# Plain w2 products in the first half-step, and modulation tiles with fixed places

## The chip, the cores and the metric

The kernel runs on one core of a Trainium2 chip. The metric is the time of one execution on the device, in microseconds. The engines are TensorE (PE, with its weight loads as PEld), VectorE (DVE), ScalarE (ACT), GpSimd (POOL, hardly used here) and SyncE (SP), whose queue issues nearly all transfers (DMAs), one after the other.

## What is computed

One layer of a diffusion trunk on 640 tokens (512 latent, 128 prompt), width D = 1024, in fp32:

```python
def swiglu(h, w1, w3, w2):
    return (silu(h @ w1) * (h @ w3)) @ w2                # F = 2816

m = (silu(cvec) @ w_ada + b_ada).reshape(-1, 9, D)       # nine modulation vectors, for c and c_ctx
x = x + 0.5 * m[2] * swiglu(rmsnorm(x, g[0]) * (1 + m[1]) + m[0], w1a, w3a, w2a)
h = rmsnorm(x, g[1]) * (1 + m[4]) + m[3]
p = h @ w_in                                             # q, k, v of attention and mLSTM, gates gm, gd
y = sigmoid(gm) * (mlstm(p) @ w_br_m) + sigmoid(gd) * (diff_attention(p) @ w_br_d)
x = x + m[5] * (y @ w_out)
x = x + 0.5 * m[8] * swiglu(rmsnorm(x, g[2]) * (1 + m[7]) + m[6], w1b, w3b, w2b)
```

The new keys and values and the final mLSTM states of the prompt are outputs too.

## The kernel before

**Numbers.** Every fp32 operand of a product is split into a high part (ACT copies it to a shorter type, `wH`, `hH`) and the rest (DVE subtracts, `wL`, `hL`), and a product is three matmuls: H x H, H x L, L x H. Tokens come in two halves of 320 (`HALF`, index `hf`), D in 8 blocks of 128, F in 11 blocks of 256 (`FB`).

**Half-steps.** After a start (norm, modulation m0 and m1, block 0 in plain products), 20 granules take blocks 1 to 10 of w1 and w3 ("up"), then 12 granules take w2 in three groups of blocks (`GROUPS`), four parts j of 256 output channels each ("down"). Every granule is a 2 x 2 product of blocks, done with 7 products instead of 8 (`HalfStep.products`): `Granule.parts` and `sums` make sums of weights (`raw<-raw`) and their splits (`wB`, `wC`, `ww`), `operand_sums` made sums of tokens, and `store_g` makes four sums of the gated tokens (`SO<-SO`), splits seven operands in two pieces (`g`, 128x1280 and 128x960) and stores them to `g_dram`, from where the down stage fetches them (`S`, `hm`, `op`) into places that become free. PE takes the products in the order in which they are written. The order of DVE, ACT and SP is made by a scheduler from that of the program and its own estimate of times; each of these engines then works strictly in its order.

**Modulation.** A vector m of 1024 channels is 8 tiles: a transfer `raw_a` of 128 x 1024 columns of w_ada, two dot products on DVE with silu(c) and silu(c_ctx) (`csil`; "ISA" or CUSTOM_DVE with a READ_ACCUMULATOR behind it), and the addition of `b_ada`. 24 tiles (m2 to m4) belong in the first half-step: 14 whole ones in the up stage (`modulation`, i = 4 to 17), 10 as two halves of 512 columns (`HalfColumns`) in the down stage, one transfer at a time. Twelve are in the attention, 12 in the branch products (`d_evac` and `m_evac`, once for each evacuated unit with mt = 1 in the first, once for each granule in the second), 8 (m8) in the second half-step (`modulation2`). The mixing's norm scale (`scale`, from m4) waits for all of the first 24.

**Mixing.** After the sum of squares (`ps_ss`) the modulated tokens go to `hH`, `hL` by block k, and PE begins with `ps_t` and `ps_g`. In the mLSTM, cells alternate with units of other products (`fill`), whose weights come through a ring of two buffers (tag `raw`) and are split a granule ahead. `w_brd`, `w_brm` (branch products, `ps_p`) and `w_out` follow; weights and modulation tiles share the ring there.

Of the kernel before, what the change touches and what calls it, by code (L numbers as in the profile page):

```python
# [16 lines left out]
D = 1024  # L17
# [14 lines left out]
def tile_trunk(ctx: ExitStack, tc: tile.TileContext, a: dict):  # L32
# [5 lines left out]
    def tt(eng, out, in0, in1, op):  # L38
        eng.tensor_tensor(out=out, in0=in0, in1=in1, op=op)  # L39
# [183 lines left out]
    GROUPS = ((0, 3), (3, 7), (7, FB))  # L223

# [3 lines left out]
    class Granule:  # L228
# [12 lines left out]
        def parts(self, fp, b12=False):  # L241
# [4 lines left out]
            E = [(self.two(fp, "C", 512, 3), hi[:, :nk])] if b12 else []  # L246
            for (h, lw), v in [(B, lo), (C, hi[:, nk:]), *E]:
# [9 lines left out]
            for i, t, o in [(A11, B, 0), (A12, B, nk * 128), (S4, C, 0), *(("b12", t, 0) for t, _ in E)]:  # L257
                self.w[i] = [[w[:, o + 128 * k : o + 128 * k + 128] for k in range(nk)] for w in t]
# [9 lines left out]

    class HalfStep:
        def __init__(self, n, fp, tmp, psum, w1, w3, w2):  # L270
# [4 lines left out]
            self.g_dram = dp.tile([7, 128, 2, FB, HALF], F32, name=f"g_dram{n}")  # L275
# [14 lines left out]
        def begin_gated(self):  # L290
            self.SO = self.fp.tile([128, 8, HALF], F32, tag="SO", name="SO")
# [4 lines left out]
        def gate_plain(self, f, hf, p):  # L296
            s = self.silu_tile(f, hf)
            act(s, p[0], AF.Silu)
            tt(vec, self.SO[:, Q[f, hf]], p[1], s, ALU.mult)
# [27 lines left out]
        def store_g(self, SO, b):  # L327

            tt(vec, SO[:, S1], SO[:, A21], SO[:, A22], ALU.add)
# [3 lines left out]
            for tag, c0, c1 in (("gA", 0, 4), ("gB", 4, 7)):  # L333
                g = self.fp.tile([128, 2, c1 - c0, HALF], F32R, tag=tag, name="g")
                act(g[:, 0], SO[:, c0:c1], AF.Copy)
                tt(vec, g[:, 1], SO[:, c0:c1], g[:, 0].bitcast(F32), ALU.subtract)
                for i in range(2):
                    nc.sync.dma_start(out=self.g_dram[c0:c1, :, i, b, :].rearrange("s p n -> p s n"), in_=g[:, i].bitcast(F32))


        def into(self, p, A, gr, i, first, w=None):

            wH, wL = gr.w[i if w is None else w]
# [10 lines left out]
        def products(self, work, between, tokens_early):  # L354
# [9 lines left out]
            for i, (gr, A, done, used) in enumerate(work):  # L364
                last = i + 1 == n

                def into(p, op, first, w=None, gr=gr, A=A, used=used):
                    self.into(p, A, gr, op, first, w)
                    if w is None:
                        used(op)  # L370

                if i + 2 < n:
                    work[i + 2][0].load()
                if not last:
                    work[i + 1][0].parts(self.fp, tokens_early and i + 2 == n)
# [4 lines left out]
                if last and tokens_early:  # L380
                    into(Z, A11, True, "b12")
                    tail[0]()
                    into(X, A12, False)
                    done(0, 0, X, None)
                    into(Z, A12, False, S4)
                    done(1, 0, Z, None)
                    tail[1]()
                    into(Y, S2, False)
                    into(Y, S3, False)
                    u3 = copy_of(Y, "nry")  # L390
                    V = acc_tile(psum)
                    into(V, S1, True)
                    done(1, 1, V, u3)
                    into(Y, A22, False)
                    done(0, 1, Y, None)
                    break
                into(Z, S1, True)
                if last:
                    p5 = copy_of(Z, "nt", 2)
                if tail:  # L400
                    tail[0]()
                if not last:
                    work[i + 1][0].sums()
                into(Y, S2, False)
# [32 lines left out]
        def up_done(self, b):  # L437
# [3 lines left out]
            def of_w1(f, hf, p, u):  # L441
                box[f, hf] = s = self.silu_tile(f, hf)
                if u is not None:
                    tt(vec, s, p, u, ALU.add)
# [3 lines left out]
            def of_w3(f, hf, p, u):  # L448
# [5 lines left out]
                tt(vec, box["SO"][:, Q[f, hf]], p, box[f, hf], ALU.mult)  # L454
                if (f, hf) == (1, 0):
# [4 lines left out]
        def run(self, x, gate, final, between, emptied=lambda: None, tokens_early=False):  # L460


            work = []
            for b in range(1, FB):
                for gr, done in zip(self.up[2 * b - 2 : 2 * b], self.up_done(b)):
                    work.append([gr, lambda i: self.ops[i], done, lambda i: None])
# [45 lines left out]
            def fetch_w2(b0, b1, j):  # L512
                def f(raw):
                    n = b1 - b0
                    for h in range(2):
                        dma(raw[:, h * n : (h + 1) * n], self.w2[b0:b1, :, h, 256 * j : 256 * j + 256].rearrange("b p n -> p b n"))
                return f

            for q, (b0, b1) in enumerate(GROUPS):
                for j in range(4):  # L520
                    work.append([Granule(b1 - b0, fetch_w2(b0, b1, j)), lambda i, q=q: at[q, i], *down_done(q, j)])
            self.products(work, between, tokens_early)


    csil_dram = dp.tile([2, D], F32, name="csil_dram")

# [1389 lines left out]
```

## Time and profile before

| | us |
|---|---|
| median of 3 runs (lowest, highest) | 1951.49 (1950.27, 1955.31) |
| profiled execution | 1950.12 |
| its span, of which PE busy | 1948.3, 1811.4 |
| first half-step up, from block 1 | 77.44 to 340.69 |
| first half-step down | 340.69 to 503.33 |
| wait of PE at the passage to the mixing | 32.5 |
| branch products | 1325.5 to 1391.5 |

The profiled execution is one of the kind that the median is made of; 1.8 us of it lie around the span. Matmuls of PE are pipelined, so a busy PE need not be PE at its best; where it is, shows in the number of matmuls that fit into a stretch.

### The profile page before, as it was taken

The page shows a single profiled execution, that of the slowest core. Times are in us where ns is not written, and L with a number is a line of the kernel's source. Part 1 is how long each engine was busy: PE and PEld are TensorE (multiplying, and loading weights), DVE is VectorE, ACT ScalarE, POOL GpSimd, SP SyncE. Part 2 cuts the span into 40 slices and gives each one's busy share as a digit, 9 for nine tenths or more (in the row PEclk, how much of TensorE's full clock was granted, in tenths as well). Part 3 has the DMA queues.
Part 4 walks back from the last instruction along what each step waited for, and adds up shares of the span by engine and source line. Part 5 has one row for each costly group of instructions (what it writes and reads, how often), then busy time and mean ns, then how long its engine had stood idle before and what let it go on. Part 6 is the DMA issues. An engine that isn't in the chain of part 4 may idle for free.

```text
span 1948.3 us, 30989 instructions
## 1 busy us (share of the span) xinstructions
PE 1811.4 (93%) x12502; PEld 1768.4 (91%) x12502; DVE 1419.9 (73%) x2480; ACT 899.1 (46%) x1537; POOL 4.9 (0%) x6
## 2 busy tenths in 40 slices
PE   6988999899398999999999989999899999999989
PEld 4888999889398998999999988899899999999989
DVE  7999888877668675675664535676666999887875
ACT  5644555433254354454453436555234545554432
POOL 1000000000000000000000000000000000000000
PEclk9899999999799999999999999999999999999999
DMA  8357555966424232133121243446643356557962
GB/s 316 138 194 241 200 179 199 396 235 220 151 78 149 69 110 94 66 104 111 67 101 59 95 163 119 142 137 225 226 143 131 113 208 233 178 181 257 385 230 100
DMA packets 144289, 328.42 MB, mean 169 GB/s; under 512 B 10321, under 2 KB 102225, under 8 KB 131345
## 3 DMA queue, kind: packets, MB, share of 16 engines
q1 hardware_dynamic: 144146, 326.44, 48.0%
q8 instruction: 98, 1.61, 0.3%
q14 instruction: 45, 0.37, 0.1%
HBM read 249.01 MB, written 77.39 MB: 168 GB/s over the span
## 4 chain that ended last, share of the span: by engine, by line
PE 68%; DVE 14%; DMA 9%; ACT 3%; issue 3%; SPq 0%; DVEq 0%; ACTq 0%
PE ps_f L52 29%; PE ps_p L52 17%; PE ps_t L52 11%; DMA raw_a<-in_w_ada_c 5%; PE sc L52 2%; PE ps_o L52 2%; DVE raw_a L559 2%; PE ps_n L52 2%; DVE raw L39 1%; DVE ww L39 1%; DMA S<-g_dram 1%; PE ps_wT L55 1%; PE ps_u L52 1%; DVE wB L39 1%; DVE junk L559 1%
## 5 line engine op out<-in xcount | busy, mean ns | idle before, releaser
L52 PE MATMUL ps_f<-S,ww 128*128 128x320 f32 x1944 | 318.7, 312 | 28.3 <-DVE ww L39 18.8
L52 PEld LDWEIGHTS ps_f<-S,ww 128*128 128x128 f32 x1944 | 295.4, 190 | 31.7 <-DVE ww L39 20.8
L52 PE MATMUL ps_p<-hH,wH 128*128 128x320 f32 x864 | 276.0, 319 | 9.7 <-DVE y L39 7.2
L52 PE MATMUL ps_p<-hL,wH 128*128 128x320 f32 x864 | 269.0, 311 | 0.0
L52 PE MATMUL ps_p<-hH,wL 128*128 128x320 f32 x864 | 268.7, 311 | 0.0
L52 PE MATMUL ps_t<-wH,hH 128*128 128x256 f32 x640 | 186.0, 291 | 32.5 <-ACT hH L201 32.5
L52 PE MATMUL ps_f<-hm,wB 128*128 128x320 f32 x1296 | 209.2, 310 | 0.2
L52 PEld LDWEIGHTS ps_f<-hm,wB 128*128 128x128 f32 x1296 | 195.6, 189 | 0.8 <-DMA hm<-g_dram 0.8
L52 PE MATMUL ps_t<-wH,hL 128*128 128x256 f32 x640 | 181.9, 284 | 0.5 <-DVE hL L42 0.5
L52 PE MATMUL ps_t<-wL,hH 128*128 128x256 f32 x640 | 181.9, 284 | 0.0
L52 PEld LDWEIGHTS ps_p<-hH,wH 128*128 128x128 f32 x864 | 164.3, 190 | 10.9 <-issue 7.4
L264 ACT ACTIVATE ww<-raw 128x2048 fp32r<-128x2048 f32 (+1 forms) x64 | 119.1, 1861 | 117.0 <-PE ps_f L52 79.7
L52 PEld LDWEIGHTS ps_p<-hL,wH 128*128 128x128 f32 x864 | 164.5, 190 | 0.6
L52 PEld LDWEIGHTS ps_p<-hH,wL 128*128 128x128 f32 x864 | 164.1, 190 | 0.0
L39 DVE TENSOR_TENSOR raw<-raw 128x512 f32<-128x512 f32 (+3 forms) x192 | 161.5, 842 | 1.6
L39 DVE TENSOR_TENSOR ww<-raw,ww 128x2048 fp32r<-128x2048 f32 (+1 forms) x64 | 142.2, 2222 | 24.4 <-ACT ww L264 24.4
L52 PEld LDWEIGHTS ps_t<-wH,hH 128*128 128x128 f32 x640 | 123.4, 193 | 33.2 <-ACT hH L201 33.0
L39 DVE TENSOR_TENSOR wL<-raw,wH 128x2048 fp32r<-128x2048 f32 x49 | 112.1, 2287 | 40.2 <-ACT wH L123 40.2
L123 ACT ACTIVATE wH<-raw 128x2048 fp32r<-128x2048 f32 x49 | 93.7, 1911 | 94.0 <-PE ps_p L52 61.2
L52 PEld LDWEIGHTS ps_t<-wH,hL 128*128 128x128 f32 x640 | 123.4, 193 | 0.8 <-DVE hL L42 0.8
L52 PEld LDWEIGHTS ps_t<-wL,hH 128*128 128x128 f32 x640 | 123.6, 193 | 0.2
L52 PE MATMUL ps_f<-hm,ww 128*128 128x320 f32 x744 | 121.8, 315 | 0.0
(284 smaller groups left out, 3379.4 us busy)
## 6 DMA issues: line engine op xcount, KB each, us to landing
g_dram<-g SPq DMA_DIRECT2D x44, 640.0 KB, 5.0
g_dram<-g SPq DMA_DIRECT2D x44, 480.0 KB, 4.8
raw_a<-in_w_ada_c SPq DMA_DIRECT2D x38, 512.0 KB, 4.7
hm<-g_dram SPq DMA_DIRECT2D x10, 1280.0 KB, 9.3
S<-g_dram SPq DMA_DIRECT2D x10, 1280.0 KB, 10.9
raw<-in_w1b SPq DMA_DIRECT2D x11, 1024.0 KB, 5.7
raw<-in_w3b SPq DMA_DIRECT2D x11, 1024.0 KB, 4.8
raw<-in_w1a SPq DMA_DIRECT2D x10, 1024.0 KB, 4.9
```

The source lines that it names most:

```text
L39: eng.tensor_tensor(out=out, in0=in0, in1=in1, op=op)
L52: tc.keep_in_program_order(nc.tensor.matmul(*args, **kw))
L55: tc.keep_in_program_order(nc.tensor.transpose(*args, **kw))
L123: act(h, raw, AF.Copy)
L264: act(t[0], flat, AF.Copy)
L559: vec.tensor_tensor_reduce(out=junk, in0=in0, in1=in1, op0=ALU.mult, op1=ALU.add, scale=1.0, scalar=0.0, accum_out=out)
```

## The change

**First half-step.** Its w2 products become plain (`Whole`, `run_whole`): 8 products of blocks instead of 7, no sums of weights there, and of gated tokens four operands (128x1280) are kept instead of seven. The groups become (0,4), (4,8), (8,11). In the last group the parts j = 1 to 3 run first on token half 0, then on half 1, and the norm of half 0 is written behind the first unit of half 1. PE has 1056 instead of 936 products of 128x320 in the down stage. A trick that took one extra split operand for the last granule (`b12`, `tokens_early`) goes.

**Modulation tiles.** `HalfColumns` goes. Each tile is tied behind one instruction on DVE (`tc.issue_after`), two loads run ahead in the first half-step, and `b_ada` is added once for 8 tiles. Places: 12 tiles in the up stage (i = 2 to 17 without multiples of 4), 12 in the down stage (i = 20 to 27), 12 in the attention as before, 12 in the mLSTM (heads 0 to 2, four cells each), 4 in the `w_brd` products, 4 in the `w_brm` products, none in the second half-step.

```diff
-    def store_g(self, SO, b):
-        tt(vec, SO[:, S1], SO[:, A21], SO[:, A22], ALU.add)
...
+            if not self.whole:
+                self.gated_sums(SO)
+            for tag, c0, c1 in (("gA", 0, 4), ("gB", 4, 7)):
+                if c0 < self.n_g:
...
+    class Whole(Granule):
+        def split(self, fp=None):
...
+            for (c0, c1, h), (_, _, lw) in zip(*t):
+                act(h, flat[:, c0:c1], AF.Copy)
+                tt(vec, lw, flat[:, c0:c1], h.bitcast(F32), ALU.subtract)
...
+            def unit(q, j, f, hf):
...
+                for kh in range(2):
+                    op = at[q][self.Q[kh, hf]]
+                    for b in range(n):
+                        w = [down[4 * q + j].w(i, n * kh + b, f) for i in range(2)]
+                        mm3(p, *w, op[:, 0, b], op[:, 1, b], kh + b == 0, kh == 1 and b == n - 1)
+                self.at_vec = add_residual(x, p, 2 * j + f, hf, gate)
...
+            for q in G:
+                last = q == G[-1]
+                for j in range(4):
+                    m = 4 * q + j
...
+                    if m + 1 < len(down):
+                        down[m + 1].split(self.fp if last and j < 2 else None)
+                    for hf in range(1 if last and j else 2):
+                        between(len(work) + m, hf)
+                        for f in range(2):
+                            unit(q, j, f, hf)
...
+            for j in range(1, 4):
+                for f in range(2):
+                    unit(G[-1], j, f, 1)
...
+        def tile(self, behind=None):
...
+                if behind is not None:
+                    st.enter_context(tc.issue_after(behind.ins))
+                for v in range(2):
+                    vec.tensor_tensor_reduce(
...
-            if at and 4 <= i < 18:
-                columns.tile()
+            if i < 20:
+                if at and 2 <= i < 18 and i % 4:
+                    columns.tile(hs.at_vec)
...
+            elif i < 28:
...
+                elif at or i % 2:
+                    columns.tile(hs.at_vec)
...
-                if hf == 1:
-                    hh2.extend(hh_tiles(hp))
-                    box["normed"] = norm2(0)
+            if (d, hf) == (2, 1):
+                hh2.extend(hh_tiles(hp))
+                box["normed"] = norm2(0)
...
+            self.at_vec = vec.reciprocal(den, den)
...
             m.cell(*st)
+            if h < 3 and n in (1, 3, 6, 8):
+                rest_of.tile(m.at_vec)
...
-            tt(vec, y1[g][:, mt, half(hf)], p, t, ALU.mult)
-            if mt == 1:
-                rest_of.tile()
+            ins = tt(vec, y1[g][:, mt, half(hf)], p, t, ALU.mult)
+            if (mt, hf) == (1, 1):
+                rest_of.tile(ins)
...
-    rest = Columns(range(48, 56))
...
-        modulation2,
+        lambda i, at: None,
```

How the rows move on DVE, first at the passage from the first half-step to the mixing. Before, the half-column tiles (ISA) stand ahead of the norm's scale:

```order
L559 ISA raw_a<-raw_a 128x512
L559 ISA raw_a 128x1
L39 TENSOR_TENSOR mod<-mod,raw_a 128x2
L42 SCALAR_TENSOR_TENSOR scale<-mod,g_norm 128x16
L42 SCALAR_TENSOR_TENSOR nt<-x,scale,ry 128x320 x2
L39 TENSOR_TENSOR wgL<-wg_raw,wgH 128x1024
L42 SCALAR_TENSOR_TENSOR hL<-nt,mod,hH 128x320 x2
```

After, the same norm stands among the residual updates of the last units, and the splits of weights and the rotary tables come behind it:

```order
L42 SCALAR_TENSOR_TENSOR nt<-x,scale,ry 128x320 x2
L42 SCALAR_TENSOR_TENSOR x<-ps_f,half_m,x 128x192
L42 SCALAR_TENSOR_TENSOR x<-ps_f,half_m,x 128x128
L42 SCALAR_TENSOR_TENSOR hL<-nt,mod,hH 128x320
L39 TENSOR_TENSOR wL<-raw,wH 128x2048
L39 TENSOR_TENSOR wgL<-wg_raw,wgH 128x1024
L42 SCALAR_TENSOR_TENSOR hL<-nt,mod,hH 128x320
L1106 COPY tab_4611<-g_qn 128x64
L39 TENSOR_TENSOR nacc<-nacc,nsq 128x320
L39 TENSOR_TENSOR ropeAq<-tab_4611,g_qn 128x256
```

The tiles and the scale (which now stands in the down stage) are gone from here; `wL` and `wgL` and the tables (`tab`, `rope`) are what is left ahead of half 1's sum of squares (`nacc`).

ACT at the same place, after. The split `wH` of the next weights and `wgH` stand behind seven of the eight pairs of `hH`:

```order
L159 ACTIVATE rt<-rv 128x320
L160 ACTIVATE ry<-rt 128x320
L201 ACTIVATE hH<-nt,mod 128x320 x7
L123 ACTIVATE wH<-raw 128x2048
L977 ACTIVATE wgH<-wg_raw 128x1024
L201 ACTIVATE hH<-nt,mod 128x320
L181 ACTIVATE nsq<-x 128x320 x5
```

Before, `wH` came ahead of the norm, and `wgH` ahead of all eight `hH`.

DVE at the end of the `w_brd` products (`y` and a number is the evacuation of a granule) and the start of `w_brm` (`ym`), before:

```order
L39 TENSOR_TENSOR y_13445<-ps_p,sig 128x320
L39 TENSOR_TENSOR wL<-raw,wH 128x2048
L39 TENSOR_TENSOR y_13445<-ps_p,sig 128x320 x2
L39 TENSOR_TENSOR wL<-raw,wH 128x2048
L559 ISA raw_a,mod<-raw_a,csil 128x1024
L559 ISA mod 128x1
```

And after:

```order
L39 TENSOR_TENSOR y_13230<-ps_p,sig 128x320 x4
L631 ISA raw_a,mod<-raw_a,csil 128x1024
L631 ISA mod 128x1
L631 ISA raw_a,mod<-raw_a,csil 128x1024
L631 ISA mod 128x1
L39 TENSOR_TENSOR wL<-raw,wH 128x2048
L39 TENSOR_TENSOR ym<-ps_p,sig 128x320
```

The fourth tile now stands between the last evacuation of `w_brd` and the first `wL` of `w_brm`, where before that `wL` came ahead of the last two evacuations.

## Rows read from the trace of the kernel before

**Rows 1.** the page, part 1: busy us (share of the span) x instructions.

```profile
PE 1811.4 (93%) x12502; PEld 1768.4 (91%) x12502; DVE 1419.9 (73%) x2480; ACT 899.1 (46%) x1537; POOL 4.9 (0%) x6
```

**Rows 2.** windows by stage, from:to, then length, busy time by engine, clock, DMA share.

```profile
77.44:503.33 425.89, 396.62 (x2619) 391.89 (x2617) 366.69 (x575) 192.47 (x267) 0.00 (x0) 0.97 0.66 234
113.00:195.00 82.00, 67.26 (x423) 65.79 (x424) 78.82 (x120) 34.98 (x49) 0.00 (x0) 0.94 0.67 228
195.00:340.69 145.69, 145.69 (x994) 145.69 (x994) 120.36 (x155) 76.83 (x106) 0.00 (x0) 1.00 0.56 192
340.69:503.33 162.64, 148.31 (x963) 145.30 (x961) 132.86 (x250) 61.27 (x86) 0.00 (x0) 0.96 0.74 268
1150.00:1325.50 175.50, 166.94 (x967) 154.07 (x968) 104.09 (x327) 100.32 (x250) 0.00 (x0) 0.96 0.50 160
1325.50:1391.50 66.00, 57.79 (x396) 57.24 (x395) 43.07 (x81) 26.00 (x32) 0.00 (x0) 0.97 0.54 193
```

**Rows 3.** PE's waits, 60 to 545 us: us in total, times, longest.

```profile
PE ps_t L52 <- ACT hH L201: 32.5, 1, 32.5
...
PE ps_f L52 <- DVE ww L39: 18.1, 7, 4.5
...
PE ps_f L52 <- DMA S<-g_dram: 3.2, 2, 2.0
```

**Rows 4.** groups of DVE by form, up stage: count, busy us, mean ns, idle before.

```profile
L559 DVE CUSTOM_DVE_ANT_0 junk<-raw_a,csil 128x1024 bf16<-128x1024 f32 x28 | 34.1, 1218 | 2.8 <-DMA raw_a<-in_w_ada_c 2.7
...
L39 DVE TENSOR_TENSOR SO<-SO 128x320 f32<-128x320 f32 x39 | 17.7, 487 | 0.4
...
L39 DVE TENSOR_TENSOR g<-SO,g 128x960 fp32r<-128x960 f32 x10 | 11.5, 1151 | 0.0
```

**Rows 5.** timeline of DVE at the passage: start us, us, instruction, idle before.

```profile
533.88 0.69 DVE L559 CUSTOM_DVE_ANT_0 raw_a<-raw_a 128x512 bf16<-128x512 f32 x1 [2.90 <-DMA raw_a<-in_w_ada_c]
...
535.55 0.17 DVE L42 SCALAR_TENSOR_TENSOR scale<-mod,g_norm 128x16 f32<-128x16 f32 x1
...
536.69 1.23 DVE L39 TENSOR_TENSOR wgL<-wg_raw,wgH 128x1024 fp32r<-128x1024 f32 x1
```

**Rows 6.** timeline of ACT at the passage.

```profile
535.60 1.06 ACT L922 ACTIVATE wgH<-wg_raw 128x1024 fp32r<-128x1024 f32 x1 [26.65 <-DVE mod L39]
```

**Rows 7.** timeline of PE at the passage.

```profile
501.53 1.92 PE L52 MATMUL ps_f<-S,ww 128*128 128x320 f32 x12
...
539.45 0.47 PE L52 MATMUL ps_g<-hH,wgH 128*128 128x320 f32 x1
...
541.92 0.70 PE L52 MATMUL ps_ss<-nacc,ones 128*128 128x320 f32 x2
...
542.75 0.52 PE L52 MATMUL ps_t<-wH,hH 128*128 128x256 f32 x1
```

**Rows 8.** timeline of ACT in the branch products.

```profile
1386.34 1.91 ACT L123 ACTIVATE wH<-raw 128x2048 fp32r<-128x2048 f32 x1 [19.52 <-DMA raw<-in_w_brm]
```

**Rows 9.** timeline of DVE in the branch products.

```profile
1388.28 2.29 DVE L39 TENSOR_TENSOR wL<-raw,wH 128x2048 fp32r<-128x2048 f32 x1 [2.18 <-ACT wH L123]
```

**Rows 10.** the page, part 6, DMA issues: count, KB each, median us to landing.

```profile
raw_a<-in_w_ada_c SPq DMA_DIRECT2D x38, 512.0 KB, 4.7
...
raw<-in_w3b SPq DMA_DIRECT2D x11, 1024.0 KB, 4.8
```

**Rows 11.** PE's waits, 545 to 1150 us.

```profile
PE ps_wT L55 <- DVE p L42: 7.0, 5, 2.6
```

**Rows 12.** PE's waits, 1320 to 1480 us.

```profile
PE ps_p L52 <- DVE y L39: 7.2, 1, 7.2
PE ps_p L52 <- DVE wL L39: 1.0, 1, 1.0
```

**Rows 13.** windows in the second half-step, columns as in rows 2.

```profile
1525.00:1625.00 100.00, 92.00 (x606) 90.50 (x607) 95.96 (x142) 50.82 (x77) 0.00 (x0) 0.98 0.61 211
1650.00:1700.00 50.00, 50.00 (x343) 50.00 (x342) 41.94 (x55) 26.91 (x37) 0.00 (x0) 1.00 0.51 177
```

More of the change, by code (lines that the diff above doesn't have):

```diff
@@ L332, in store_g, with into @@
             tt(vec, SO[:, S4], SO[:, A12], SO[:, S2], ALU.subtract)
[L333 to L343, printed above, removed]
+        def into(self, p, A, gr, i, first):
+            wH, wL = gr.w[i]
             n, a = gr.nk, A(i)
@@ L352, in copy_of, with products @@
             return t
-        def products(self, work, between, tokens_early):
+        def products(self, work, between, then=()):
             n = len(work)
@@ L365, in products, with into @@
                 last = i + 1 == n
[L367 to L370, printed above, removed]
+                def into(p, op, first, gr=gr, A=A, used=used):
+                    self.into(p, A, gr, op, first)
+                    used(op)
                 if i + 2 < n:
                     work[i + 2][0].load()
+                elif then:
+                    then[i + 2 - n].load()
                 if not last:
-                    work[i + 1][0].parts(self.fp, tokens_early and i + 2 == n)
+                    work[i + 1][0].parts(self.fp)
                 between(i, 0)
@@ L379, in products @@
                 act(Y, X, AF.Copy)
[L380 to L396, printed above, removed]
                 into(Z, S1, True)
                 if last:
-                    p5 = copy_of(Z, "nt", 2)
+                    p5 = copy_of(Z, *(("nrv",) if then else ("nt", 2)))
                 if tail:
@@ L403, in products @@
                     work[i + 1][0].sums()
+                elif then:
+                    then[0].split()
                 into(Y, S2, False)
@@ L468, in run @@
+        def run(self, x, gate, final, between, emptied=lambda: None):
+            work = self.up_work()
             at = {(0, i): self.ops[i] for i in range(7)}
@@ L522, in run, with __getitem__ @@
-            self.products(work, between, tokens_early)
+                    work.append([Granule(b1 - b0, self.fetch_w2(b0, b1, j)), lambda i, q=q: at[q, i], *down_done(q, j)])
+            self.products(work, between)
     csil_dram = dp.tile([2, D], F32, name="csil_dram")
+    class Two(list):
+        def __getitem__(self, idx):
+            return list.__getitem__(self, idx[1])
     class Columns:
         def __init__(self, tiles):
-            self.todo, self.then, self.next = list(tiles), {}, None
@@ L533, in place @@
-        def place(self, csil, load, ahead=True):
-            self.csil, self.load, self.ahead = csil, load, ahead
+            self.todo, self.then, self.next, self.left = list(tiles), {}, [], {}
+            for n in self.todo:
+                self.left[n // 8] = self.left.get(n // 8, 0) + 1
+        def place(self, n, csil, load, ahead=2):
+            self.n, self.csil, self.load, self.ahead = n, csil, load, ahead
             self.fetch()
         def fetch(self):
-            if self.todo:
-                gi, i = divmod(self.todo[0], 2)
-                self.next = self.load(a["w_ada_c"][gi, :, i])
@@ L543, in tile @@
-        def tile(self, fetch=True):
-            if not self.todo:
-                return
-            n, (raw, junk) = self.todo.pop(0), self.next
-            if fetch and self.ahead:
-                self.fetch()
-            ct = 16 + n
-            for v in range(2):
-                dot(junk, raw, self.csil[:, v, :], mod[:, ct, v : v + 1])
-            ts(mod[:, ct, :], mod[:, ct, :], b_ada[:, ct : ct + 1], ALU.add)
-            if fetch and not self.ahead:
-                self.fetch()
-            if n in self.then:
-                self.then[n]()
@@ L1601, in tile_trunk @@
         steps += [(4, d, d == 1, False, True) for d in range(2)]
-        for st, then in zip(steps, later):
+        for n, (st, then) in enumerate(zip(steps, later)):
             if st[0] == 4 and st[1] == 0 and h < 3:
```

233 lines of the change are left out of this document (120 added, 113 removed).

## The prediction

> **What bounds the kernel now.** TensorE (PE) is busy 1811.4 us of a span of 1948.3 us [rows 1], so I look for the places where it isn't. The windows by stage give PE's busy time and its count of matmuls [rows 2]. From 195.00 to 340.69 us it runs 994 matmuls in 145.69 us without a gap: 146.6 ns for one 128x320 product, the price of a product wherever PE is the bound. From 77.44 to 503.33 us, the half-step behind its first block, the program has 20 x 84 + 936 = 2616 products. At that price they are 383.4 us; the stretch lasts 425.89 us, so 42.5 us are lost. The table of waits says to what [rows 3]: weight operands from VectorE (DVE), `ww`, 18.1 us in seven waits, fetched gated tokens, `S`, 3.2 us; the rest is smaller waits and slow clock behind the gaps (0.94 in 113 to 195, where PE is busy only 67.26 of 82.00 us). DVE is busy 78.82 us of those 82: modulation tiles sit between the weight operands. The single largest wait is 32.5 us, at the passage to the mixing.
>
> **First half-step, products up.** 14 modulation tiles go through this stretch, two dot products of 1218 ns each [rows 4], about 2.5 us a tile, packed into consecutive granules. After the change 12 tiles stand there, three in four granules, each behind a named instruction. The gated sums go too (4 x 0.487 us a block) and the second split of g (1.151 us): 3.1 us less for DVE in each block of two granules, that is in 24.6 us of PE. In four granules, 49.3 us of PE, DVE then has 40.7 us of work as it has without tiles (120.36 / 145.69 [rows 2]), less 6.2, plus 7.4 for three tiles: 41.9. So DVE is no longer the bound. I take 1 us of PE loss there instead of 17.0 (263.25 us from 77.44 to 340.69, less 1680 x 0.1466); between 0 and 6, as a single tile can still delay one `ww`.
>
> **Products down.** Before, 162.64 us for 936 products, 137.2 us of bare work: 25.4 lost. After, 8 plain products take the place of 7 made with sums: 1056 x 0.1466 = 154.8 us, 17.6 more. What belonged to the seven products goes: the sums of weights, the extra split operands, the additions behind PSUM. What stays for DVE in a granule of 96 products (14.1 us) is one split of 2.29 us (as [rows 9]), four residual updates and at most two tiles (5 us), so PE should be the bound. I take 2 us lost (0 to 10: the first fetches of g still come while the last up granule frees their places, and were waited for 3.2 us before). Both parts: 2736 x 0.1466 + 3 = 404.0 us against 425.89, **gain 21.9**.
>
> [...]
>
> **Passage to the mixing.** Before, the last product ends at 503.45 us and the products on block 2 of the mixing operand begin at 542.75 [rows 7], 39.3 us later. In between DVE runs five half-column tiles, each waiting about 3 us for its load (the last at 533.88: 2.90), and only then the scale of the norm at 535.55 [rows 5]; ACT's split `wgH` had waited 26.65 us for it [rows 6]. After, all 24 tiles are done in granules 2 to 27, and the norm of token half 0 stands beside the last five units of products (5 x 18 x 0.1466 = 13.2 us), which are half 1. So the wait on the scale goes. What is late next: in the order of ACT `wH` and then `wgH` stand behind the very last product, whose end is T, because they take the buffer of the last w2 granule; DVE follows with `wL` and `wgL`. T + 1.91 [rows 8] + 2.29 [rows 9] + 1.23 [rows 5] = T + 5.4 us. Then come products as before from 539.45 to the sum of squares at 541.92 [rows 7], 2.5 us, T + 8; but the additions for that sum of half 1 now stand among the rotary tables on DVE, and these wait for loads behind the store of x. One load of 4.7 us [rows 10] gives T + 12.7. Bounds T + 8 and T + 18 (two loads). Gain 39.3 - 12.7 = **26.6** (21 to 31).
>
> **mLSTM.** 12 tiles come in: 29.7 us of DVE in a stretch of 175.50 us where DVE is busy 104.09 and PE 166.94 [rows 2]. By share they fit. But DVE is in the chain of each cell, and a tile behind a reciprocal delays what follows by up to 2.5 us. In the attention, where 12 tiles stand before and after, PE waited 7.0 us on one DVE operand [rows 11], 0.6 us a tile at most. I take 0.3 a tile, since PE has fill units between cells: **cost 3.5** (0 to 13, a full 1.1 each). The weight loads that now wait for a tile's buffer are used two cells later or more.
>
> **Branch products.** Before, 66.00 us for 384 products of 0.1466: 9.7 lost, of it 7.2 and 1.0 in two waits [rows 12]. The 7.2 is the load of `w_brm`, which waits for one of two buffers that tiles hold too; then `wH` at 1386.34 [rows 8] and `wL` at 1388.28 [rows 9]. After, there are 4 tiles instead of 8, but each is tied behind the last evacuation of its granule. In the order of DVE tile 4 stands behind the last evacuation of the fourth granule and ahead of the first `wL` of `w_brm`, and the load takes the buffer that tile 4 gives back: 0.5 + 2.5 for evacuation and tile, 4.8 for the load [rows 10], 1.91 + 2.29 for the split are 12 us in which PE has nothing. The granule before has the same chain behind the loads of z, some 19 us under 14.1 us of products: 5 us where 1.0 was. 17 + 0.7 of slow clock against 9.7: **cost 8** (0 to 12).
>
> **Second half-step.** From 1525 to 1625 us PE is busy 92.00 of 100 while DVE runs its 8 tiles (95.96); from 1650 on, without tiles, PE is busy 50.00 of 50.00 with DVE at 41.94 [rows 13]. After, no tiles: **gain 7** of the 8 (3 to 9).
>
> The rest (attention, end of the second half-step and its waits for g) keeps its instructions. **Sum:** 21.9 + 26.6 + 7 - 3.5 - 8 = 44.0 us. The profiled execution took 1950.1; less 44.0 is 1906.1. The median of the runs lies 1.4 us above that execution: 1907.5.
>
> **Rivals.** (a) *The passage waits again.* If the rotary tables hold the last sum of squares for three loads or more, block 2 starts at T + 25, the gain shrinks to 14.3, the time is 1920. For it: the store of x, the table loads and the splits meet there. Against: loads of that size land in 4.7 us [rows 10].
> (b) *The down stage keeps its stalls.* If fetches of g, 1.3 MB each, still cost the 25.4 us of before, 22 us are lost against the forecast: 1930. For it: a DMA share of 0.74 in that stretch [rows 2]. Against: the operands of g fall from 7 to 4.
> (c) *The tied tiles cost nothing* in mLSTM and branch products: 1907.5 - 11.5 = 1896. For it: PE waits little in mLSTM now. Against: the order of DVE puts tile 4 ahead of `wL`.
> (d) *Slower: a tied tile at the head of DVE waits for its load*, and all behind it waits too, weight operands among them. The half-column tiles did just that, about 3 us each [rows 5]. If the 24 tiles of the first half-step did so with PE waiting, 72 us would come on: 1980. From 1.8 us a tile on the gain is gone. Against it: two loads run ahead, 9 to 12 us lie between tiles, and a load lands in 4.7. [...]
> (e) *PE is the bound of the first half-step after all*: the added products are paid in full and the stalls stay under other names, a cost of 17.6 instead of a gain of 21.9: 1947. Against it: the clean stretch from 195 us on, where DVE has no tiles.
>
> **Chances.** Forecast 0.55 (1898 to 1917), (a) 0.13, (b) 0.12, (c) 0.13, (d) 0.04, (e) 0.03. The range takes in (a) and (c), and (b) to its middle: 1890 to 1930. Faster by over 0.3% (5.9 us, about what can be told from no change) 0.92, within it 0.04 ((e), and (a) with (b)), slower 0.04.
>
> **What would show it.** In the trace of the changed kernel: PE at 146.6 ns a product from 113 us to the end of the half-step; no wait over 10 us at the passage, the first idle there ending on `wgL` or `wL`; a wait of about 12 us ahead of the first `w_brm` product and of about 5 a granule earlier; PE full where the second half-step had tiles; mLSTM at most 5 us longer. Wrong would make it: tiles idle for `raw_a` in the first half-step (d), waits for S or hm in the down stage (b), a passage of over 20 us (a).

## The result and the profile after

The changed kernel takes 1918.33 us (median of 4 runs, 1918.09 to 1921.42), the kernel before, run beside it, 1950.88. The ratio is 0.9832, 95% interval 0.9814 to 0.9851: 32.6 us faster, where 44.0 were forecast; the forecast of 1907.5 was 10.8 us too low, inside its range of 1890 to 1930. The span of the profiled execution falls from 1948.3 to 1916.7 us. The page's first part, which answers [rows 1]:

```profile
PE 1822.1 (95%) x12622; PEld 1780.8 (93%) x12622; DVE 1329.9 (69%) x2244; ACT 855.1 (45%) x1469; POOL 4.9 (0%) x6
```

PE has 120 matmuls more and is busy 10.7 us more, while DVE lost 90.0 us of work. The stages, from the first matmul of each to that of the next on PE's timeline (T is the end of the last product of the first half-step):

| stage, us | before | after | forecast of the difference | measured |
|---|---|---|---|---|
| start, to block 1 | 77.4 | 78.3 | 0 | +0.9 |
| first half-step, block 1 to T | 426.0 | 407.5 | -21.9 | -18.5 |
| passage, T to block 2 of the mixing operand | 39.3 | 12.9 | -26.6 | -26.4 |
| attention, to the first cell of the mLSTM | 617.7 | 618.9 | 0 | +1.2 |
| mLSTM, to the first w_brd product | 165.0 | 163.4 | +3.5 | -1.6 |
| w_brd, to the first w_brm product | 66.0 | 81.1 | +8 | +15.1 |
| w_brm and w_out, to the second half-step | 115.2 | 122.2 | 0 | +7.0 |
| second half-step, to the end | 441.5 | 432.4 | -7 | -9.1 |
| span | 1948.3 | 1916.7 | -44.0 | -31.6 |

The windows of the stages, which answer [rows 2] (up, down, mLSTM, w_brd, the first part of w_brm, w_brm with w_out; from:to, length, busy time with counts by engine, granted clock, share of DMA, GB/s):

```profile
78.34:325.88 247.54, 247.19 (x1682) 246.41 (x1681) 200.43 (x253) 119.83 (x169) 0.00 (x0) 1.00 0.57 192
325.88:485.86 159.98, 156.66 (x1062) 155.55 (x1060) 95.25 (x163) 33.85 (x37) 0.00 (x0) 1.00 0.58 208
1117.63:1281.05 163.42, 156.56 (x921) 143.21 (x919) 124.45 (x366) 95.48 (x245) 0.00 (x0) 0.99 0.59 191
1281.05:1362.16 81.11, 61.11 (x396) 60.02 (x395) 33.60 (x58) 28.90 (x33) 0.00 (x0) 0.89 0.49 180
1362.16:1380.00 17.84, 16.41 (x95) 16.02 (x96) 8.81 (x11) 3.22 (x4) 0.00 (x0) 0.82 0.28 90
1362.16:1484.61 122.45, 119.18 (x774) 117.43 (x775) 77.65 (x132) 44.27 (x66) 0.00 (x0) 0.96 0.41 139
```

The up stage ends here with its 1680th product, at 325.88, and the kernel before is cut in the same way under e3. It lasts 247.54 us, 1.3 more than 1680 products at 146.6 ns, and PE is busy 247.19 of it: the loss there is nearly gone, with DVE busy 200.43 us. The mLSTM carries 12 tiles more on DVE, 124.45 us of work against 101.64 in the same stage of the kernel before, and is no longer for it:

```profile
1160.45:1325.49 165.04, 158.25 (x920) 145.38 (x918) 101.64 (x322) 98.16 (x245) 0.00 (x0) 0.97 0.49 155
```

In the w_brd stage 20.0 of 81.11 us are idle. PE's waits from 70 to 560 us, and from 1110 to 1490 us (us in total, times, longest), which answer [rows 3] and [rows 12]:

```profile
PE ps_ss L52 <- DVE nacc L39: 3.2, 1, 3.2
PE ps_f L52 <- DMA hm<-g_dram: 2.1, 1, 2.1
PE ps_g L52 <- DVE wgL L39: 2.0, 1, 2.0
PE ps_f L52 <- DMA S<-g_dram: 1.2, 1, 1.2
PE ps_g L52 <- ACT wgH L977: 1.0, 1, 1.0
PE ps_t L52 <- DVE x L42: 0.9, 1, 0.9
```

```profile
PE ps_p L52 <- ACT wH L123: 17.0, 2, 13.5
PE ps_p L52 <- DVE wL L39: 6.2, 4, 1.8
...
```

No `ww` is left in the first list, and the 32.5 us are gone too. In the second the two waits of [rows 12], 7.2 and 1.0, have become 17.0 and 6.2.

The passage on DVE and on PE, which answers [rows 5] and [rows 7] (start, us, instruction, idle before):

```profile
487.75 2.29 DVE L39 TENSOR_TENSOR wL<-raw,wH 128x2048 fp32r<-128x2048 f32 x1 [0.72 <-ACT wH L123]
489.96 1.22 DVE L39 TENSOR_TENSOR wgL<-wg_raw,wgH 128x1024 fp32r<-128x1024 f32 x1
...
493.25 0.43 DVE L39 TENSOR_TENSOR ropeAq<-tab,g_qn 128x256 f32<-128x256 f32 x1 [1.11 <-DMA tab<-in_cos]
...
496.39 0.48 DVE L39 TENSOR_TENSOR nacc<-nacc,nsq 128x320 f32<-128x320 f32 x1
```

```profile
483.79 2.07 PE L52 MATMUL ps_f<-op,ww 128*128 128x320 f32 x13
...
496.93 1.43 PE L52 MATMUL ps_ss<-nacc,ones 128*128 128x320 f32 x2 [3.17 <-DVE nacc L39]
...
498.77 0.88 PE L52 MATMUL ps_t<-wH,hH 128*128 128x256 f32 x1
```

T is 485.86. `wgL` ends at 491.18, T + 5.3 (forecast T + 5.4). The sum of squares waits 3.17 us for the additions between the rotary tables, the last at 496.39; the tables had waited 1.11 us for their load, and the second addition, whose squares ACT had done by 492.6, stood behind them in DVE's order until 494.27. The sum of squares begins at T + 11.1 and block 2 at T + 12.9 (forecast T + 12.7).

The end of the w_brd products, on DVE, SP and ACT, which answers [rows 8] and [rows 9]:

```profile
1348.67 0.49 DVE L39 TENSOR_TENSOR y<-ps_p,sig 128x320 f32<-128x320 f32 x1 [3.03 <-PE ps_p L52]
1349.07 1.22 DVE L631 CUSTOM_DVE_ANT_0 raw_a<-raw_a,csil 128x1024 bf16<-128x1024 f32 x1
1350.21 0.08 DVE L631 DVE_READ_ACCUMULATOR2_ANT mod<- 128x1 f32 x1
1350.33 1.23 DVE L631 CUSTOM_DVE_ANT_0 raw_a<-raw_a,csil 128x1024 bf16<-128x1024 f32 x1
1351.48 0.08 DVE L631 DVE_READ_ACCUMULATOR2_ANT mod<- 128x1 f32 x1
1362.14 2.29 DVE L39 TENSOR_TENSOR wL<-raw,wH 128x2048 fp32r<-128x2048 f32 x1 [10.58 <-ACT wH L123]
```

```profile
1328.96 3.14 SPq L74 DMA_DIRECT2D raw_a<-in_w_ada_c  x2
1345.58 2.03 SPq L1724 DMA_DIRECT2D x<-x_dram  x4
1349.18 0.79 SPq L74 DMA_DIRECT2D sig<-gm_dram  x2
1351.59 13.20 SPq L74 DMA_DIRECT2D raw<-in_w_brm  x2
```

```profile
1360.20 1.91 ACT L123 ACTIVATE wH<-raw 128x2048 fp32r<-128x2048 f32 x1 [1.20 <-DMA raw<-in_w_brm]
```

The last evacuation is at 1348.67, tile 4 ends at 1351.5, the load of `w_brm` is issued at 1351.59, and ACT begins to split it at 1360.20: 8.6 us for a load priced at 4.8. The loads of x (1345.58) and of the gates (1349.18), some 4 MB, were issued just ahead of it. PE has nothing from 1348.6 to 1362.16.

The first line of SP shows why the load could not come sooner. It holds the loads of two tiles, 4 and 5; tile 5's was issued at 1331.78, as soon as the last `w_brd` weights were split and their buffer was free. From then on tiles held both buffers of the ring. Tile 4 gave its buffer back at 1351.5; tile 5 runs at 1382 to 1386 only, so the first two loads of `w_brm` went through one buffer, the second 12.9 us behind the first.

### The profile page after: what moved, and what is told of

It is laid out like the page before. It is cut to its first block, busy times and chain, and to the rows that moved or that the text cites. A ratio compares the mean times of both kernels' runs of the same rounds, so it can differ in the third digit from the quotient of the medians.

```text
span 1916.7 us, 30755 instructions
## 1 busy us (share of the span) xinstructions
PE 1822.1 (95%) x12622; PEld 1780.8 (93%) x12622; DVE 1329.9 (69%) x2244; ACT 855.1 (45%) x1469; POOL 4.9 (0%) x6
## 4 chain that ended last, share of the span: by engine, by line
PE 83%; DVE 7%; DMA 6%; ACT 2%; issue 1%; SPq 1%; DVEq 0%; ACTq 0%
PE ps_f L52 41%; PE ps_p L52 19%; PE ps_t L52 11%; PE sc L52 2%; PE ps_o L52 2%; PE ps_n L52 2%; DVE wL L39 1%; PE ps_wT L55 1%; PE ps_u L52 1%; PE ps_qkT L55 1%; DMA hm<-g_dram 1%; ACT wH L123 1%; DMA raw<-in_w_brm 1%; DMA raw<-in_w_brd 1%; DMA S<-g_dram 1%
## 5 line engine op out<-in xcount | busy, mean ns | idle before, releaser
L52 PE MATMUL ps_f<-S,ww 128*128 128x320 f32 x2052 | 329.7, 310 | 4.8 <-DMA S<-g_dram 2.5
L52 PEld LDWEIGHTS ps_f<-S,ww 128*128 128x128 f32 x2052 | 308.5, 188 | 6.4 <-ACT wC L250 2.2
L52 PE MATMUL ps_p<-hH,wH 128*128 128x320 f32 x864 | 276.4, 320 | 16.0 <-ACT wH L123 13.5
L52 PE MATMUL ps_f<-hm,wB 128*128 128x320 f32 x1128 | 181.7, 310 | 0.2 <-DMA hm<-g_dram 0.2
L52 PEld LDWEIGHTS ps_f<-hm,wB 128*128 128x128 f32 x1128 | 170.0, 188 | 0.4 <-DMA hm<-g_dram 0.4
L52 PEld LDWEIGHTS ps_p<-hH,wL 128*128 128x128 f32 x864 | 164.7, 191 | 4.7 <-DVE wL L39 4.7
L52 PEld LDWEIGHTS ps_p<-hL,wH 128*128 128x128 f32 x864 | 165.0, 191 | 0.5
L39 DVE TENSOR_TENSOR ww<-raw,ww 128x2048 fp32r<-128x2048 f32 (+1 forms) x62 | 138.7, 2237 | 29.5 <-ACT ww L265 17.6
L52 PE MATMUL ps_f<-hm,ww 128*128 128x320 f32 x996 | 156.9, 310 | 2.1 <-DMA hm<-g_dram 2.1
L52 PEld LDWEIGHTS ps_f<-hm,ww 128*128 128x128 f32 x996 | 149.3, 189 | 2.4 <-DMA hm<-g_dram 2.4
L39 DVE TENSOR_TENSOR raw<-raw 128x1024 f32<-128x1024 f32 (+2 forms) x156 | 132.5, 851 | 1.9
L265 ACT ACTIVATE ww<-raw 128x2048 fp32r<-128x2048 f32 (+1 forms) x52 | 97.7, 1880 | 61.2 <-PE ps_f L52 59.5
```

The costliest lines, as they stand in the source:

```text
L39: return eng.tensor_tensor(out=out, in0=in0, in1=in1, op=op)
L52: tc.keep_in_program_order(nc.tensor.matmul(*args, **kw))
L265: act(t[0], flat, AF.Copy)
```

## The experiments

All ran beside the kernel before; times are given as ratios to it. The stages of each, on the same marks:

| us | first half-step | passage | attention | mLSTM | w_brd | w_brm, w_out | second | span |
|---|---|---|---|---|---|---|---|---|
| before | 426.0 | 39.3 | 617.7 | 165.0 | 66.0 | 115.2 | 441.5 | 1948.3 |
| after | 407.5 | 12.9 | 618.9 | 163.4 | 81.1 | 122.2 | 432.4 | 1916.7 |
| e1 no branch tiles | 407.4 | 12.9 | 619.0 | 160.8 | 58.2 | 113.8 | 434.0 | 1883.5 |
| e2 tiles in mLSTM | 408.5 | 12.8 | 617.7 | 178.8 | 62.7 | 113.8 | 433.8 | 1906.4 |
| e3 before without 24 | 395.7 | 13.9 | 619.6 | 162.8 | 63.3 | 115.5 | 440.1 | 1888.2 |
| e4 after without 24 | 404.1 | 12.9 | 619.2 | 162.5 | 80.7 | 121.7 | 431.7 | 1911.1 |
| e5 untied | 417.3 | 12.8 | 619.5 | 163.0 | 81.7 | 122.3 | 433.0 | 1927.4 |
| e6 gated sums back | 419.4 | 13.2 | 618.6 | 164.7 | 80.8 | 121.5 | 432.0 | 1928.5 |
| e7 tiles in attention | 406.7 | 9.6 | 622.2 | 163.5 | 58.2 | 113.8 | 433.3 | 1884.5 |
| e8 tiles in heads 0 to 2 | 408.6 | 9.5 | 616.1 | 169.9 | 58.2 | 113.8 | 433.0 | 1887.0 |
| e9 norm at the end | 407.8 | 13.7 | 618.9 | 165.8 | 80.1 | 121.6 | 433.9 | 1919.8 |

Stages that an edit doesn't touch differ by 1 to 3 us between runs; smaller differences are not read.

**e1: the tiles of the branch products left out.**

```diff
-                self.next.append(self.load(a["w_ada_c"][gi, :, i]))
...
+                self.next.append(None if n >= 48 else self.load(a["w_ada_c"][gi, :, i]))
...
-                for v in range(2):
+                for v in range(0 if n >= 48 else 2):
```

> The changed kernel with the eight tiles of the branch products left out, transfers and dot products (m8 is then wrong); all else stays. In the changed kernel the stretch from the first w_brd product to the first w_brm product lasts 81.1 us (66.0 before), and from there to the second half-step 122.5 us (115.5 before). Theory A (tiles and weights take turns in two buffers, and each tile is tied behind the last evacuation of a granule): the first stretch falls to 57 to 60 us, the second to 114 to 116, the time by 28 to 31 us to about 1888. Rival B (the loads of z, x and the branch gates crowd the queue there, with or without tiles): the first stretch stays above 72 us, the second above 119, the time above 1905.

Ratio 0.9678 (0.9662 to 0.9694). Against the changed kernel 31.3 us are gone in two stages: 22.9 in the w_brd stage and 8.4 behind it. The w_brd stage as a window:

```profile
1277.48:1335.71 58.23, 57.55 (x397) 57.29 (x395) 24.75 (x41) 25.70 (x31) 0.00 (x0) 1.00 0.44 162
```

PE is busy all of it but one wait of 0.7 us. Theory A holds (the second stretch came out at 113.8, just under its 114 to 116): the eight tiles, 20 us of work for DVE, which has 24.75 us of other work in these 58.23 us, cost 31 us of PE. Of the 22.9, 20.0 are waits (1.2, 3.5, 1.8 and 13.5 us); the other 2.9, and 5.2 of the 8.4 (two waits of 1.4 and 1.8 make the rest), go with the slow clock behind the waits, as two windows of the changed kernel show beside the one above from 1362.16 to 1380:

```profile
1329.48:1348.60 19.12, 17.36 (x96) 16.86 (x96) 3.74 (x4) 0.00 (x0) 0.00 (x0) 0.82 0.27 83
1432.60:1450.00 17.40, 17.38 (x108) 17.38 (x109) 9.48 (x13) 6.16 (x8) 0.00 (x0) 0.90 0.68 233
```

Behind the 3.5 and the 13.5 us of waiting the granted clock is 0.82 on average, with 0.50 from 1332 to 1338 (23 matmuls in 6.00 us) and from 1362.16 to 1368, and 1.00 from 1338 to 1348.6 (73 in 10.60 us) and from 1370 to 1380, so PE was for about a third of that time at 0.50; behind the wait of 1.8 us at 1432.6 it is 0.90, with 0.51 from 1434 to 1437, so a fifth.

The ring of two is not the whole of it. Of the 12 tiles that the kernel before has for these products, none of them tied, ten ran in these two stages through the same ring (two dot products each):

```profile
L559 DVE CUSTOM_DVE_ANT_0 raw_a<-raw_a,csil 128x1024 bf16<-128x1024 f32 x20 | 24.3, 1221 | 12.9 <-DMA raw_a<-in_w_ada_c 12.8
```

It needed 66.0 + 115.2 us for them against 172.0 here: 9 us for ten tiles, where eight tied ones cost 31. As far as two kernels that differ elsewhere can tell, what is dear is a buffer held from a tile's early load to its late place. No run has these eight tiles untied, or a third buffer.

**e2: the same tiles moved into the mLSTM, five a head.**

```diff
-            if h < 3 and n in (1, 3, 6, 8):
+            if n in (1, 3, 5, 6, 8):
                 rest_of.tile(m.at_vec)
...
             ins = tt(vec, y1[g][:, mt, half(hf)], p, t, ALU.mult)
-            if (mt, hf) == (1, 1):
-                rest_of.tile(ins)
```

> The changed kernel with the eight tiles of the branch products moved into the mLSTM: five cells in each of four heads carry a tile (20 instead of 12), none in the branch products. Nothing is left out. Theory A: the branch stretches as without tiles (57 to 60 and 114 to 116 us), the mLSTM at most 4 us longer than the 163.4 us of the changed kernel, the time about 1890. Rival B: head 3, in which DVE also splits the attention's output and the two buffers carry its loads, waits for the tiles: mLSTM 8 to 15 us longer, the time 1898 to 1905.

Ratio 0.9792 (0.9776 to 0.9808). The second branch stretch falls as A said, the first to 62.7 us, a little above its 57 to 60; but the mLSTM stage grows by 15.4 us. That is nearly B's number (8 to 15), but not quite its place: 13.7 us are one wait at the very end, for the first weights of the branch products. PE's wait, and DVE and SP around it:

```profile
PE ps_p L52 <- ACT wH L123: 13.7, 1, 13.7
```

```profile
1277.99 1.23 DVE L631 CUSTOM_DVE_ANT_0 raw_a<-raw_a,csil 128x1024 bf16<-128x1024 f32 x1 [1.39 <-DMA raw_a<-in_w_ada_c]
...
1280.41 0.08 DVE L631 DVE_READ_ACCUMULATOR2_ANT mod<- 128x1 f32 x1
...
1296.06 2.29 DVE L39 TENSOR_TENSOR wL<-raw,wH 128x2048 fp32r<-128x2048 f32 x1 [4.39 <-ACT wH L123]
```

```profile
1280.52 0.33 SPq L74 DMA_DIRECT2D raw<-in_w_brd  x1
```

The last tile waited 1.39 us for its own load and ended at 1280.41; the load of `w_brd` is issued at 1280.52, in the buffer that it gave back, and ACT, busy without a gap from 1281.31, begins to split it at 1294.13 only. The same hold-up as ahead of `w_brm`, at another place.

**e3: the kernel before without the 24 tiles of the first half-step.**

```diff
+            if self.todo[0] < 24:
+                n = self.todo.pop(0)
+                if n in self.then:
+                    self.then[n]()
+                return
...
-            self.csil, self.junk, self.raw, self.then = csil, junk, raw, then
-            self.fetch()
+            then()
+            self.todo = []
```

> The kernel before with the 24 tiles of the first half-step left out, whole and half-column ones (m2 to m4 are then wrong); sums of gated tokens and seven-product w2 stay. Theory A (the tiles on DVE were the loss): up stage from 263.3 to about 247 us, down stage from 162.6 to 140 to 145, passage from 39.3 to 10 to 16 us, the time about 1885 to 1892, which would mean that plain w2 products with their 17.6 us were not needed. Rival B (the sums of weights and of gated tokens were the loss in the down stage): up stage 247 to 252 all the same, down stage 154 to 162, the time 1900 to 1910.

Ratio 0.9714 (0.9693 to 0.9734). PE's waits, 60 to 545 us:

```profile
PE ps_t L52 <- ACT hH L202: 7.0, 1, 7.0
PE ps_f L52 <- DMA S<-g_dram: 3.7, 2, 2.0
PE ps_f L52 <- ACT ww L265: 3.2, 1, 3.2
...
PE ps_f L52 <- DVE ww L39: 1.4, 1, 1.4
```

The half-step falls by 30.3 us, the passage by 25.4. For the two parts of the half-step both kernels have to be cut at the same product. The mark at 340.69 in the kernel before is its first product down, but 24 products of the last granule up run after it. Cut at the 1680th product, before and in this run:

```profile
77.44:344.21 266.77, 251.83 (x1682) 250.10 (x1681) 236.66 (x331) 132.06 (x183) 0.00 (x0) 0.98 0.62 215
344.21:503.45 159.24, 144.91 (x939) 141.90 (x938) 130.15 (x244) 60.53 (x85) 0.00 (x0) 0.96 0.73 265
```

```profile
77.28:323.67 246.39, 246.39 (x1682) 246.39 (x1681) 205.00 (x260) 132.15 (x183) 0.00 (x0) 1.00 0.58 203
323.67:472.98 149.31, 140.83 (x939) 139.44 (x938) 112.59 (x176) 61.52 (x85) 0.00 (x0) 0.98 0.70 260
```

At 146.6 ns a product the kernel before loses 20.5 us up and 22.1 us down. Without the tiles 0.2 and 12.1 are left: they made 20.4 us of the loss up and 9.9 of the loss down, and the rest down (`S`, `ww`, slow clock) stays without them. The down stage, 149.3 us, lies between the theories, as does the gain (0.9714 is 56 us, and A's times were 59 to 66 below the kernel before).

**e4: the changed kernel without those 24 tiles.** As e1, with `n < 24` for `n >= 48`.

> The changed kernel with the 24 tiles of the first half-step left out (m2 to m4 are then wrong). It shows what the tied tiles still cost. Theory A: nothing on TensorE's path in the up stage, and of the 3.3 us waited for fetched g at the start of the down stage up to 3, as csil and the first tiles' loads stand ahead of those fetches: the time 1915 to 1918. Rival B: the tied tiles delay weight operands a little everywhere: the time 1905 to 1912.

Ratio 0.9828 (0.9814 to 0.9843), not to be told from the changed kernel's. In the half-step the spans differ by 3.4 us, about what A gives: 2.2 us of it are shorter waits for fetched g. Beside e3 this run has the price of the edit to the products of the half-step where no tile is in the way: 404.1 against 395.7 us, **8.4 us dearer**, nearly all of it in the down stage, 157.43 against 149.31 us:

```profile
324.88:482.31 157.43, 156.38 (x1062) 155.54 (x1060) 67.31 (x112) 33.60 (x37) 0.00 (x0) 1.00 0.47 167
```

Of the 17.6 us of added products about 9 come back, as the plain stage loses 2.7 us and the one of seven products 12.1.

**e5: the 24 tiles untied.**

```diff
                 if at and 2 <= i < 18 and i % 4:
-                    columns.tile(hs.at_vec)
+                    columns.tile()
...
                 elif at or i % 2:
-                    columns.tile(hs.at_vec)
+                    columns.tile()
```

> The changed kernel with the 24 tiles of the first half-step no longer tied: same places in the program, same loads, but the scheduler may move them. In its order of DVE the 12 tiles of the up stage then stand in some five granules on end, two or three a granule, instead of three in four granules. Theory A (with 9.0 us of other work in a granule of 12.3 us, DVE can carry one tile of 2.5 us, not two or three): waits for ww come back in the up stage, 8 to 15 us from 78 us to the end of the products, the time 1926 to 1934. Rival B (it is the missing gated sums, not the ties, that made room): waits under 3 us, the time within 4 of the changed kernel's 1918.

Ratio 0.9893 (0.9869 to 0.9916). The half-step is 9.8 us longer, all of it in the up stage. Two windows of 25 us, columns as above:

```profile
125.00:150.00 25.00, 20.57 (x123) 20.05 (x122) 24.66 (x36) 8.89 (x12) 0.00 (x0) 0.86 0.55 195
200.00:225.00 25.00, 25.00 (x173) 25.00 (x172) 18.33 (x23) 12.38 (x18) 0.00 (x0) 1.00 0.39 140
```

Where the scheduler packs the tiles DVE is full and PE has 123 matmuls at a clock of 0.86; later, with none left, DVE has 18.33 us of work and PE is full. This is theory A.

**e6: the gated sums' work back.**

```diff
-            self.SO = self.fp.tile([128, 8, HALF], F32, tag="SO", name="SO")[:, : self.n_g]
+            self.SO_full = self.fp.tile([128, 8, HALF], F32, tag="SO", name="SO")
+            self.SO = self.SO_full[:, : self.n_g]
...
             if not self.whole:
                 self.gated_sums(SO)
+            else:
+                full = self.SO_full
+                for s in range(4):
+                    tt(vec, full[:, 4 + s], SO[:, s], SO[:, 3 - s], ALU.add)
+                g = self.fp.tile([128, 2, 3, HALF], F32R, tag="gB", name="g")
+                act(g[:, 0], full[:, 4:7], AF.Copy)
+                tt(vec, g[:, 1], full[:, 4:7], g[:, 0].bitcast(F32), ALU.subtract)
```

> The changed kernel with the work of the gated sums put back beside it, for each block of the up stage four additions of 128x320 and a split of 128x960 on ACT and DVE; their results are not used. The tiles stay tied. DVE then has 48.1 us of work in four granules of 49.3 us instead of 41.9. Theory A (the places of the tiles are what matters): up stage longer by 0 to 3 us, the time 1918 to 1922. Rival B (DVE needs the room that the sums gave up): waits for ww of 5 to 12 us, the time 1924 to 1930.

Ratio 0.9899 (0.9881 to 0.9917). The edit puts back the work on DVE and ACT, not the stores. The half-step is 11.9 us longer, 10.8 of it in the up stage, with the ties in place; PE's waits on the operand from 70 to 480 us:

```profile
PE ps_f L52 <- DVE ww L39: 8.0, 6, 2.4
```

This is theory B. So neither the ties nor the missing sums would have done alone what the change does in the up stage: each without the other gives back 10 to 11 us of the 19 won there.

**e7: the branch tiles into the attention, and the rotary tables behind the additions.**

```diff
-            if hd < 6 and qi in (1, 3):
+            if hd < 6 and (qi in (1, 2, 3) or qi == 4 and hd < 2):
                 rest_of.tile()
...
-                tt(vec, self.acc, self.acc, sq, ALU.add)
+                self.added = tt(vec, self.acc, self.acc, sq, ALU.add).ins
...
-    with tc.issue_after(normed2):
+    with tc.issue_after(stats[1].added):
```

The two calls `rest_of.place` get 20 and 12 instead of 12 and 20, and the branch products lose their tiles as in e2.

> The changed kernel with two edits. The eight tiles of the branch products move into the attention, which then has 20 tiles, untied; and the rotary tables' work on DVE is tied behind the last addition for half 1's sum of squares. Theory A (only the ring of two buffers beside short weight loads is dear; the attention has DVE at 64% and time): attention 2 to 8 us longer, branch stretches 58 and 114, as without tiles; block 2 at the passage at T + 10 instead of T + 12.9; the time 1890 to 1896. Rival B (the attention's own chain, scores to weights through DVE, takes each added tile in full): attention 20 us longer, the time about 1905; for the passage, that the load of the tables is late anyway: T + 12.9.

1886.75 us, ratio 0.9689 (0.9674 to 0.9703). The attention takes eight tiles more for 3.3 us against the changed kernel, 6.1 against e8, which has the same tables and 12 tiles there; the branch stages are those of e1. This is theory A. At the passage (PE's waits, 480 to 505 us):

```profile
PE ps_g L52 <- DVE wgL L39: 2.0, 1, 2.0
...
PE ps_ss L52 <- DVE nacc L39: 0.5, 1, 0.5
```

the wait on the sum of squares is 0.5 instead of 3.2 us and block 2 begins at T + 9.6. Nothing is left out in this kernel: with e8, whose interval overlaps its own, it is the best of the study, 3.1% ahead of the kernel before and 32 us by the span ahead of the changed one.

**e8: six tiles in each of heads 0 to 2, two in head 3.**

```diff
-            if h < 3 and n in (1, 3, 6, 8):
+            if n in ((0, 1, 3, 5, 6, 8) if h < 3 else (0, 1)):
                 rest_of.tile(m.at_vec)
```

Tables and branch products as in e7.

> As the run before in the passage, but the eight tiles go into the mLSTM: six cells in each of heads 0 to 2, and the first two in head 3, so that no tile stands near the first load of w_brd. With five tiles in head 3 that load was waited for 13.7 us. Theory A (it was the two buffers, held by tiles and by the attention's output when w_brd was wanted): no such wait, mLSTM 163 to 170 us, branch stretches 58 and 114, the time 1888 to 1895. Rival B (DVE in the mLSTM is full with six tiles a head): mLSTM 175 or more, the time above 1898.

Ratio 0.9701 (0.9687 to 0.9716). mLSTM 169.9 us, 6.5 more than in the changed kernel and 8.9 less than in e2, though it holds as many tiles as e2: what was dear there was the place beside the load of `w_brd`. This is theory A.

**e9: the norm of half 0 behind all products.**

```diff
-            if (d, hf) == (2, 1):
+            if (d, hf) == (7, 1):
                 hh2.extend(hh_tiles(hp))
                 box["normed"] = norm2(0)
```

> The changed kernel with the norm of token half 0 written behind the last unit of half 1 instead of the first, so that no product covers it. It tells what of the 26.4 us won at the passage belongs to the order by token halves and what to the tiles being done in time. The kernel before without its 24 tiles had block 2 at T + 13.9, without any cover. Theory A (the tiles were the whole wait; norm, splits and tables run beside each other): block 2 at T + 13 to T + 17 instead of T + 12.9, the time 1918 to 1923. Rival B (the cover of 13.2 us is used in full): block 2 at T + 22 to T + 26, the time 1927 to 1932.

Ratio 0.9852 (0.9827 to 0.9877), which takes in the changed kernel's 0.9832. PE's one wait there:

```profile
PE ps_t L52 <- ACT hH L201: 6.9, 1, 6.9
```

PE now waits for the first `hH` instead of `wgH`, `wgL` and the sum of squares, and block 2 begins at T + 13.7, 0.8 us later. This is theory A. But 0.8 us is not the whole worth of the cover: the wait of 3.2 us on the sum of squares is gone here as well, as the tables stand behind the norm in DVE's order. Beside e7, where the tables are out of the way too (T + 9.6), the norm without its cover costs 4.1 us.

## Why the prediction was right, and where its terms were wrong

The sign, the range and the order of the gains held. By its steps:

- **Up stage.** Right in size: 1.3 us lost, 1 forecast. Right in cause, as far as it said that DVE would have 42 of 49 us to do; e5 and e6 show that both halves of that sum were needed. The loss before was 20.5 us, not 17.0: the sum took 1680 products ahead of 340.69, and 24 of them run behind it. The down stage's loss is smaller by as much, 22.1 and not 25.4, so the sum of both holds.
- **Down stage.** 160.0 us, 0.8 of it the sum of squares of half 0, against 154.8 and 2 forecast: some 3 us over, as long as the waits for `hm` and `S` (2.1 and 1.2). The step that failed is the attribution: I gave all of the loss to "what belonged to the seven products". By e3 9.9 of the 22.1 us were the half-column tiles; the other 12.1 did belong to the seven products, and plain ones lose 2.7 (e4), which is less than the 17.6 us that they add. By themselves they cost 8.4 us in the half-step. What they give is room and DVE time: with the tied tiles there, the work on DVE and ACT that went with them is worth 11.9 us (e6). No run has seven products with tied tiles, so whether the plain ones were needed is not settled.
- **Passage.** Forecast T + 12.7, measured T + 12.9, by the links named (`wH`, `wL`, `wgL`, then the additions among the tables), but the close fit is in part luck. The term of 4.7 us stood for one load of the tables; they waited 1.11 us for it, and the 3.17 us of PE's wait are mostly DVE's own work on tables and additions. And the sum stopped at the start of the sum of squares, which it put at T + 12.7 and which came at T + 11.1; its products, which the sum left out, took 1.8 us more. The first two waits there, 0.9 and 1.0 us, were on `x` and `wgH` and not on `wL` or `wgL`. The cover of 13.2 us by token halves, which the text counted as one reason, matters little: e9 loses 0.8 us without it, 4.1 beside e7, and e3 had T + 13.9. Nearly all of the 26.4 us come from the other reason, the tiles done in time.
- **mLSTM.** Cost 3.5 forecast, nothing to be seen (163.4 against 165.0). No run leaves out these 12 tiles alone. Eight more there cost 6.5 us in e8, 0.8 a tile, so the place is not free in general.
- **Branch products.** The mechanism was right, down to the place (tile 4 ahead of the first `wL`, and a shorter wait a granule earlier: 5 us forecast, 3.5 + 1.8 measured). The size was wrong twice: the load of `w_brm` took 8.6 us, not 4.8, since I took its price from the median of another stretch and not from what stands ahead of it in SP's queue (x and the gates); and 7.0 us behind the first `w_brm` product were not counted at all. They are two waits, of 1.4 and 1.8 us, for `wL` (both gone in e1), and the slow clock, for which I had 0.7 us in all, an estimate that no row shows; e1 puts 2.9 + 5.2 us in its place. Together 22.1 us where 8 were forecast and 12 was the bound: these 14.1 us are more than the miss of 12.4 by the span; the other stages cancel to 1.7.
- **Second half-step.** 7 forecast, 9.1 measured. From 1507 to 1700 us, where DVE has its tiles, PE of the kernel before waits for `ww` three times, and the changed kernel, from 1485 to 1700, not once. The change also moved the loads of x there ahead, which no run tests by itself. The wait before:

```profile
PE ps_f L52 <- DVE ww L39: 6.8, 3, 2.6
```

- **The rivals.** (a) and (b) did not come: passage 12.9, down loss 5.2. (c) is refuted for the branch products and true for the mLSTM. (d) did not come: the 24 tiles cost 3.4 us in all (e4), 2.2 of it in waits for fetched g. (e) holds for a part: the added products are paid to about half (8.4 of 17.6 us), but the stalls did go. In the half-step as a whole the tiles on DVE made 30.3 of the 42.6 us lost (e3).

## What to carry to other kernels

Side work that is cheap by its engine's share is priced by the buffer it holds, and for how long: eight tied tiles of 2.5 us on a half-idle engine (DVE busy 33.60 of the 81.11 us of w_brd) cost 31 us, since each held one of two buffers that the next weights needed from its load to its place, and 3 to 6 us in the attention. So price such a tie by the chain behind it (last evacuation, tile, load, two splits) against the products that cover it, take the load's price from what is queued ahead of it at that place, and add the slow clock where it follows a wait (2.9 and 5.2 us here; none behind the 2.1 us for `hm`). And when a change does several things for one gain, price each alone: here the tile places and the lighter DVE earned the up stage only together, the token halves earned little, and the plain products cost time by themselves.

## What the runs showed of the hardware

A load of 1 MB took 8.6 us with some 4 MB of others issued on the same queue in the 6 us before it; the median of eleven such loads is 4.8 [rows 10]. That the others are the cause is read from the order and not tested alone; in the kernel before the two loads of `w_brm` issued ahead of those of x (1381.48 and 1385.5) took 4.8 and 4.9 us, the third, issued at 1394.75 behind the same six and a tile's, 10.6. From 1350 to 1358 in the changed kernel the DMA share is 1.03 at 425 GB/s. After a wait of 13.5 us PE lost 2.5 us more: 95 matmuls in the 16.41 us it was busy, where 112 fit at 146.6 ns, with the granted clock at 0.82 on average. Not every wait had that behind it: from 325.88 to 345, where PE waited 2.1 us for `hm` and 1.2 for `S`, the clock is 1.00.
